# Order and pace of four instruction streams in a two-layer hybrid attention and recurrence block

## The chip, the cores and the metric

The kernel runs on one core of a Trainium2 chip, in one launch. The metric is the device time of that launch in microseconds; a profiled execution gives the span from the first to the last instruction, and every engine's instructions in it.

## What is computed

Two layers run over 512 latent tokens and 256 context tokens of width 1024, in float32. Each layer normalises and modulates the tokens, multiplies them by one wide input matrix, and hands its columns to three groups of heads: latent attention (`mla`), differential attention (`diff`), and a gated recurrence in both directions. The heads' outputs are joined, go through an output matrix, and a gated feed-forward block (`swiglu`) follows.

```python
for l in range(DEPTH):
    h = modulate(rms_norm(x, g_norm1[l]), sh1, sc1)
    fl = stream_features(h, lw, rope)          # h @ w_in, split into head groups
    ...
    mix_l, mix_c = token_mixers(fl, fc, lw, lam, lam_init, with_ctx_out)
    x = x + gt1 * (mix_l @ w_out[l])
    h2 = modulate(rms_norm(x, g_norm2[l]), sh2, sc2)
    x = x + gt2 * swiglu(h2, w_ffn_gate[l], w_ffn_up[l], w_ffn_down[l])
return rms_norm(x, g_final)
```

Layer 0 computes outputs for all 768 tokens, layer 1 for the 512 latent tokens alone; layer 1's keys, values and recurrence states still cover the context.

## The kernel before

Each matrix product is three matmuls (high by high, high by low, low by high part), so every weight block is loaded, copied into its high part on ScalarE (line 102) and subtracted into its low part on VectorE (line 105).

A layer's first phase, `phase_a`, is written as four generators that each put out a few instructions and then yield a cost:

- `g` (`stream_g`): the projections, in the order of a string in `G_ORDER`. `t0` to `t3` are three projections each (forward gate, backward gate, query; called HF, HB and HQ below) that feed head pair 0 to 3 of the recurrence; `h0` and `h1` are the recurrence's values (line 504), `h0` for pairs 0 and 1, `h1` for pairs 2 and 3; `q` is the four blocks of the differential queries and keys, `d` its values; `g0` to `g3` are the output gates of the four pairs; `a4` to `a9` are blocks of the modulation matrix. After the last of them the stream goes on with the output projection, once the recurrence is done.
- `h` (`stream_hh`): the recurrence, two heads side by side (`s` = 0 and 1), four pairs one after another. A pair goes through seven levels (lines 931, 944, 972, 982), then transposes its keys (line 1005), forms chunk states with the values (line 1013), multiplies out (line 1035) and normalises (line 248). The output tiles of a pair wait for its values (`h0` or `h1`). If the pair's gate is there, the pair multiplies it in; else it stores its result in `scr_n`, and the gate step loads it and multiplies.
- `p` (`stream_p`): the low-rank queries, keys and values of latent attention.
- `a` (`stream_a`): attention, which begins where `p` ends. An item is 128 queries of a head: scores (line 775), a reduction (line 779), exponentials, transposes (line 815), and after each two heads a product with the values (line 829). Layer 0 has the units context `mla`, latent `mla` 0, context `diff`, latent `diff` 0, latent `mla` 1, latent `diff` 1, in this order; layer 1 has the latent four.

The streams are interleaved by a virtual clock. `PRM[l]` is the place where `p` begins, and the pace of `g`, `h`, `p` and `a`:

```python
while gens:
    k = min(gens, key=lambda n: vt[n])
    try:
        tc.cur_priority -= AHEAD[l].get(k, 0)
        c = next(gens[k])
        tc.cur_priority += AHEAD[l].get(k, 0)
    ...
    if c == "wait":
        vt[k] = min(vt[o] for o in gens if o != k) + 1e-3
    else:
        vt[k] += c * stretch[k]
```

An instruction's place in this writing order is its priority: of the instructions that are ready by the framework's own costs, the one with the lowest number goes first on its engine, so a late one may still run early as filling. `AHEAD` lowers the number of a stream's instructions by so many places. The matmuls of the levels and of the product with the values have their number lowered by 1000 apart from that. The engines then run their queues in the order so fixed; all loads and stores share SyncE's queue.

The output projection of a layer runs in two batches of tokens (first and second), and its tile `xT` takes the room that the recurrence's tiles leave. The first batch needs the recurrence and the attention of its own tokens; the second batch needs all attention. The feed-forward block behind it does not depend on the strings that change.

Of the kernel before, what the change touches and what calls it, by code (L numbers as in the profile page):

```python
# [31 lines left out]
GROUPS = ((4, 4, 4, 4, 3, 3), (4, 4, 4, 4, 3, 3))  # L32
LEVELS = (1, 2, 4, 8, 16, 32, 64)
PRED = (1, 2, 4, 8, 16)
G_ORDER = ("t0 h0 q t1 d t2 h1 t3 a5 a4 g0 a8 a6 g1 a9 a7 g3 g2", "t0 t1 h0 t2 q d h1 t3 g0 g1 g3 g2")


PRM = ((40, 2, 2.1, 2, 1.2), (45, 1.8, 2.7, 2.2, 0.4))


NQ, NA = 8, 4
# [16 lines left out]
RUSH = 1000  # L58
RUSH2 = 1000
TRB = 0  # L60
AHEAD = ({}, {})
NSTEP = "011"


# [31 lines left out]
def build(tc, I, out):  # L96
# [310 lines left out]
    def hpair():  # L407
        return (hp.tile([128, KT, T], F32R, tag="hh", name="hh"), hp.tile([128, KT, T], F32R, tag="hl", name="hl"))
# [13 lines left out]
    def phase_a(l, h, fs):  # L422
# [92 lines left out]
        def stream_g():  # L515
# [72 lines left out]
            for i in range(2):  # L588
                steps[f"h{i}"] = partial(hi, i)
            for key in G_ORDER[l].split():  # L590
                yield from steps[key]()
# [518 lines left out]
        with ps:  # L1110
            vt = {"g": 0.0, "h": 0.0, "p": PRM[l][0], "a": 1e9}
            apool = ExitStack()
            gens = {"g": stream_g(), "h": stream_hh(),
                    "p": stream_p(apool.enter_context(tc.tile_pool(name=f"P{l}", bufs=1, reuse_waits="tile")))}
            stretch = dict(zip("ghpa", (PRM[l][i] for i in (1, 2, 3, 4))))
# [6 lines that stand above are left out]
                except StopIteration:  # L1122
# [17 lines left out]

    FIRST = {"q": [O_DQ, O_DQ + 128, O_DK], "t": [O_HF, O_HB, O_HQ]}[G_ORDER[0][0]]
    h = hpair()
# [114 lines left out]
    for l in range(DEPTH):  # L1257
# [4 lines left out]
        with ExitStack() as fs:  # L1262
# [9 lines left out]
            def ada_next():  # L1272
                for ll, nb in [(0, 10), (0, 11)] + [(1, nb) for nb in range(12)]:
                    if f"{'ab'[ll]}{nb}" in " ".join(G_ORDER).split():
                        continue
# [332 lines left out]
```

## Time and profile before

| what | before |
| --- | --- |
| median of 3 runs | 2206.95 us (2202.46 to 2211.0) |
| the profiled execution | 2209.03 us, its span 2206.9 us |
| mean granted TensorE clock in it | 0.944 |
| PE busy | 2032.4 us, 92% |
| DVE busy | 1605.8 us, 73% |
| ACT busy | 1060.0 us, 48% |

PE is TensorE's matmuls, DVE is VectorE, ACT is ScalarE, SP is SyncE. "Busy" counts time in which an engine had an instruction of its own in work. The granted clock is a share of full speed, averaged over a stretch. The profiled execution's time is 2.1 us over its span, and 2.1 us over the median.

### The profile page before, as it was taken

Reading aid. Unit: us, or ns where it says so; the run is one execution under the profiler, and the core shown is the slowest. Engines: PE = TensorE matmul, PEld = TensorE weight load, DVE = VectorE, ACT = ScalarE, POOL = GpSimd, SP = SyncE. Lnnn points to the kernel's source line nnn. Section 1 sums busy time; section 2 is a strip of 40 time slices with the busy share of each in tenths; the row PEclk is TensorE's granted clock in tenths of the full one; section 3 lists DMA queues with packets and bytes.
Section 4 is the critical chain, followed back from the end, with each engine's and each line's share of the span. In section 5 each row is a group of like instructions: output and inputs, shape, how many; then the busy total and the mean of one; then the engine's idle time right before and its main releaser. Section 6 shows DMA issues by size and latency. Waiting matters only on the chain. (4 is left out here: it accounts for less than half of the span.)

```text
span 2206.9 us, 38015 instructions
## 1 busy us (share of the span) xinstructions
PE 2032.4 (92%) x14863; PEld 1759.1 (80%) x14863; DVE 1605.8 (73%) x3395; ACT 1060.0 (48%) x1871; POOL 13.1 (1%) x48
## 2 busy tenths in 40 slices
PE   7999899888898999999999999978988699999998
PEld 4887778666678888999999878757866489899997
DVE  5574597888657565797776776798568668877787
ACT  4433778565654323232333454445677444344443
POOL 0000000000000000000000000000000000000000
PEclk7999999888999999999999999989988589999999
DMA  9426744455765424464322333354645263333321
GB/s 318 122 77 165 196 131 131 128 164 170 223 203 167 125 86 153 129 187 132 118 70 68 118 114 102 95 150 128 171 129 163 83 204 98 96 105 101 103 85 68
DMA packets 321243, 296.51 MB, mean 134 GB/s; under 512 B 28875, under 2 KB 263721, under 8 KB 321065
## 3 DMA queue, kind: packets, MB, share of 16 engines
q1 hardware_dynamic: 321064, 294.10, 45.5%
q8 instruction: 117, 1.92, 0.4%
q14 instruction: 62, 0.50, 0.1%
HBM read 241.09 MB, written 52.95 MB: 133 GB/s over the span
## 5 line engine op out<-in xcount | busy, mean ns | idle before, releaser
L102 ACT ACTIVATE whi<-wst 128x1024 fp32r<-128x1024 f32 (+2 forms) x248 | 225.1, 908 | 399.9 <-PE f L195 146.4
L105 DVE TENSOR_TENSOR wlo<-wst,whi 128x1024 fp32r<-128x1024 f32 (+2 forms) x248 | 256.0, 1034 | 80.3 <-ACT whi L102 77.3
L195 PE MATMUL q<-hh,whi 128*128 128x384 f32 (+1 forms) x708 | 222.9, 317 | 4.3 <-ACT whi L102 3.2
L195 PE MATMUL q<-hh,wlo 128*128 128x384 f32 (+1 forms) x708 | 221.2, 315 | 0.9 <-DVE wlo L105 0.9
L195 PE MATMUL q<-hl,whi 128*128 128x384 f32 (+1 forms) x708 | 221.7, 314 | 0.0
L195 PE MATMUL g<-hh,whi 128*128 128x512 f32 (+1 forms) x560 | 199.6, 359 | 10.2 <-ACT zt L102 5.0
L195 PE MATMUL g<-hh,wlo 128*128 128x512 f32 (+1 forms) x560 | 197.8, 355 | 2.1 <-DVE wlo L105 2.1
L195 PE MATMUL g<-hl,whi 128*128 128x512 f32 (+1 forms) x560 | 198.9, 357 | 0.7 <-DVE hl L108 0.5
L195 PE MATMUL f<-ah,whi 128*128 128x512 f32 (+1 forms) x380 | 137.3, 364 | 5.3 <-DVE xT L108 4.1
L779 DVE TENSOR_REDUCE mx<-b 128x1 f32<-128x768 f32 (+1 forms) x120 | 101.5, 848 | 55.3 <-PE b L775 54.4
L195 PEld LDWEIGHTS q<-hh,whi 128*128 128x128 f32 x708 | 134.3, 190 | 9.1 <-ACT whi L102 5.1
L195 PE MATMUL f<-ah,wlo 128*128 128x512 f32 (+1 forms) x380 | 136.1, 361 | 1.1 <-DVE wlo L105 1.1
L195 PE MATMUL f<-al,whi 128*128 128x512 f32 (+1 forms) x380 | 136.5, 361 | 0.0
L108 DVE SCALAR_TENSOR_TENSOR xT<-f,mod,xT 128x256 f32<-128x256 f32 (+1 forms) x164 | 85.9, 546 | 69.1 <-PE f L195 68.5
L195 PEld LDWEIGHTS q<-hh,wlo 128*128 128x128 f32 x708 | 134.3, 190 | 1.7 <-DVE wlo L105 1.6
L195 PEld LDWEIGHTS q<-hl,whi 128*128 128x128 f32 x708 | 134.7, 191 | 0.3
L195 PEld LDWEIGHTS g<-hh,whi 128*128 128x128 f32 x560 | 108.1, 193 | 26.6 <-ACT zt L102 6.1
L102 ACT ACTIVATE kz<-KK 64x384 f32<-64x384 f32 (+1 forms) x192 | 91.3, 476 | 76.1 <-DVE KK L972 55.9
L775 PE MATMUL b<-k,q 96*128 96x256 f32 x352 | 100.5, 399 | 25.8 <-DMA q<-scr_d 15.6
L195 PEld LDWEIGHTS g<-hh,wlo 128*128 128x128 f32 x560 | 107.4, 192 | 17.2 <-DVE wlo L105 3.3
L195 PE MATMUL g<-T,whi 128*128 128x384 f32 (+1 forms) x544 | 121.1, 311 | 0.0
L195 PE MATMUL g<-m,whi 128*128 128x256 f32 (+1 forms) x512 | 117.2, 323 | 4.2 <-ACT acc L102 2.0
(308 smaller groups left out, 5021.2 us busy)
## 6 DMA issues: line engine op xcount, KB each, us to landing
wst<-in_w_in_dram SPq DMA_DIRECT2D x58, 512.0 KB, 5.3
wa<-in_w_ada_dram SPq DMA_DIRECT2D x56, 512.0 KB, 3.8
wst<-in_w_out_dram SPq DMA_DIRECT2D x32, 512.0 KB, 5.5
wst<-in_w_ffn_down_dram SPq DMA_DIRECT2D x64, 256.0 KB, 2.9
wst<-in_w_ffn_gate_dram SPq DMA_DIRECT2D x26, 512.0 KB, 3.7
wst<-in_w_ada_dram SPq DMA_DIRECT2D x24, 512.0 KB, 4.9
hin<-scr_z SPq DMA_DIRECT2D x48, 192.0 KB, 3.4
k<-scr_k SPq DMA_DIRECT2D x16, 576.0 KB
```

Of the source, the lines that this page charges most:

```text
L102: return S.activation(out=out, in_=in_, func=func, **kw)
L105: eng.tensor_tensor(out=out, in0=in0, in1=in1, op=op)
L108: return V.scalar_tensor_tensor(out=out, in0=in0, scalar=scalar, in1=in1, op0=op0, op1=op1)
L195: PE.matmul(out=o, lhsT=x[:, k, ms], rhs=y[:, k, cols], start=start and k == 0 and p == 0, stop=stop and k == nk - 1 and p == 2, skip_grou ...
L775: PE.matmul(out=s[:, 256 + k0:256 + k0 + kn], lhsT=qq[:, q0:q0 + 128], rhs=kk[:, k0:k0 + kn], start=p == 0, stop=p == len(passes) - 1)
L779: V.tensor_reduce(out=mx, in_=sv, axis=AX.X, op=ALU.min)
```

## The change

It sets other constants: the order of the `g` steps in both layers, the pace of `g` and `a` in layer 0, the place where `p` begins in layer 1, and `AHEAD`, which was empty. In layer 0 `h0` moves behind `q` and `t1`, and the gates and modulation blocks at the end change places. In layer 1 `h0` moves in front of `t1`, and `g3` in front of `t3`. Attention's instructions are numbered 80 places earlier in layer 0 and 40 in layer 1, those of layer 1's recurrence 40 places later. Every computation stays.

```diff
-G_ORDER = ("t0 h0 q t1 d t2 h1 t3 a5 a4 g0 a8 a6 g1 a9 a7 g3 g2", "t0 t1 h0 t2 q d h1 t3 g0 g1 g3 g2")
-
-
-PRM = ((40, 2, 2.1, 2, 1.2), (45, 1.8, 2.7, 2.2, 0.4))
+G_ORDER = ("t0 q t1 h0 d t2 h1 t3 a8 a5 a4 a6 g1 a9 g0 a7 g2 g3", "t0 h0 t1 t2 q d h1 g3 t3 g0 g1 g2")
+
+
+PRM = ((40, 2.4, 2.1, 2, 0.91), (35, 1.8, 2.7, 2.2, 0.4))
...
-AHEAD = ({}, {})
+AHEAD = ({'h': 0, 'a': 80}, {'a': 40, 'h': -40})
```

## Rows read from the trace of the kernel before

**Rows 1.** The page's first part: busy time, share, instructions.
```profile
PE 2032.4 (92%) x14863; PEld 1759.1 (80%) x14863; DVE 1605.8 (73%) x3395; ACT 1060.0 (48%) x1871; POOL 13.1 (1%) x48
```

**Rows 2.** Stretches of both first phases; columns in the first line.
```profile
core 0: us, PE busy (x) PEld busy (x) DVE busy (x) ACT busy (x) POOL busy (x), PEclk, DMA share, GB/s
165.00:250.00 85.00, 75.11 (x415) 59.92 (x414) 41.63 (x64) 37.58 (x68) 0.00 (x0) 0.98 0.71 180
...
400.00:550.00 150.00, 123.97 (x1237) 91.76 (x1237) 124.19 (x304) 91.69 (x170) 0.58 (x4) 0.84 0.54 159
...
618.00:708.00 90.00, 83.83 (x485) 70.86 (x485) 65.12 (x148) 44.25 (x78) 0.00 (x0) 0.94 0.55 171
...
1690.00:1766.00 76.00, 47.98 (x352) 37.04 (x353) 53.77 (x137) 40.27 (x79) 0.03 (x1) 0.63 0.32 96
1766.00:1829.00 63.00, 58.19 (x441) 55.04 (x441) 41.74 (x92) 27.88 (x45) 0.00 (x0) 0.91 0.61 186
```

**Rows 3.** Timeline of layer 1 on PE, around h1's end and the output projection's start.
```profile
1577.08 0.28 PE L504 MATMUL g<-whi,hl 128*128 128x256 f32 x1
...
1594.55 0.39 PE L1035 MATMUL c<-QQ,sb 128*64 128x128 f32 x4
...
1752.42 1.97 PE L248 MATMUL c<-ident,rs_y 128*64 128x128 f32 x16 [1.53 <-DVE rs_y L108]
...
1766.36 0.63 PE L195 MATMUL g<-m,whi 128*128 128x256 f32 x2
```

**Rows 4.** Timeline of layer 0: HQ1's end, starts of pairs 1 and 2, last normalisation.
```profile
243.34 0.69 DVE L108 SCALAR_TENSOR_TENSOR zt<-zt,g 128x512 f32<-128x512 f32 x1 [3.43 <-ACT zt L102]
...
260.95 1.17 DVE L972 TENSOR_TENSOR KK<-KK,hin 64x384 f32<-64x384 f32 x2 [0.26 <-PE c L931]
...
356.50 0.96 DVE L105 TENSOR_TENSOR QQ<-hin 128x768 f32<-128x768 f32 x1 [1.11 <-DMA hin<-scr_z]
...
578.58 1.53 PE L248 MATMUL c<-ident,rs_y 128*64 128x128 f32 x24
```

**Rows 5.** Timeline of layer 0, products with the values: four of them.
```profile
412.23 1.08 PE L829 MATMUL b<-pt,v 128*64 128x256 f32 x8 [0.33 <-ACT pt L102]
...
522.16 2.81 PE L829 MATMUL b<-pt,v 128*64 128x256 f32 x24
...
613.30 4.55 PE L829 MATMUL c<-pt,v 128*64 128x256 f32 x24
...
651.77 2.81 PE L829 MATMUL c<-pt,v 128*64 128x256 f32 x24
```

**Rows 6.** Timeline of SP's queue before layer 0's output projection.
```profile
617.89 0.34 SPq L411 DMA_DIRECT2D v<-scr_w  x1
618.27 0.95 SPq L411 DMA_DIRECT2D m<-scr_m  x2
```

**Rows 7.** Groups by line on PE, 618 to 708 us: attention's share.
```profile
L815 PE MATMUL c<-ident,P 128*128 128x128 f32 x24 | 3.3, 274 | 0.0
L829 PE MATMUL c<-pt,v 128*64 128x256 f32 x24 | 2.8, 383 | 0.0
L775 PE MATMUL b<-zt 96*128 96x256 f32 (+1 forms) x8 | 1.9, 341 | 0.0
L775 PE MATMUL b<-k,q 96*128 96x256 f32 (+1 forms) x6 | 1.8, 375 | 0.0
```

**Rows 8.** What PE waited for, 165 to 250 us: total, times, longest.
```profile
PE b L195 <- DVE zt L105: 5.4, 5, 2.2
...
PE g L195 <- ACT zt L102: 3.5, 2, 2.4
```

**Rows 9.** Stretch 400 to 550 us, line 779's reductions alone; columns us, DVE, clock, DMA.
```profile
400.00:550.00 150.00, 19.35 (x21) 0.84 0.54 159
```

**Rows 10.** The page's DMA issues: KB each, median us to landing.
```profile
hin<-scr_z SPq DMA_DIRECT2D x48, 192.0 KB, 3.4
...
scr_z<-zt SPq DMA_DIRECT2D x19, 384.0 KB, 2.4
```

## The prediction

> **What bounds the kernel now.** The page's busy times come first: PE is busy for 92% of the span, but 2206.9 less 2032.4 us still leaves 174 us without a matmul [rows 1]. Where they lie is read from the stretches. In layer 0 PE is idle for 26 of 150 us between 400 and 550, at a mean clock of 0.84, with DVE busy for 124 of the 150. In layer 1 it is idle for 28 of 76 us between 1690 and 1766, at 0.63 [rows 2]. A mean of 0.63 lies between the two levels of 1.2 and 2.4 GHz; (1 − 0.63) × 2, three quarters of that stretch, ran at the low one. So the first phases lose time twice, to idle PE and to the clock behind it, and both stand where recurrence and attention run out of projections that could fill.
>
> What ends each first phase is read from the timeline, backwards. In layer 1 the output projection starts at 1766.4, 13.9 us behind the last normalisation of the recurrence at 1752.4. The recurrence in its turn was held up at `h1`: its last matmul is at 1577.1, and the pair that had waited multiplies out 17.5 us later [rows 3]. In layer 0 the same tie holds to HQ: pair 1 starts 17.6 us behind the step that closes HQ1 (260.95 less 243.34), pair 2 starts on a load of `scr_z`. The recurrence is thus paced by the projections that feed it, and its last normalisation is at 578.6 [rows 4]. Attention in layer 0 is slower than it could be: between 412 and 522 two pairs of heads of the latent `diff` unit take 55 us each, and the last pair, from 613.3 to 651.8, takes 38.5 [rows 5]. It is still running when the output projection starts, and it delays that start: SP's queue takes the load of the last operands `m` behind a load for attention, at 618.3 [rows 6]. So layer 0's output projection starts at about 618, some 39 us behind the normalisation, where layer 1 needs 14.
>
> **The change, step by step.** The number of instructions and transfers is the same; only order moves. Working through the virtual clock gives the new order of writing. In layer 0 HQ3 stands behind 168.6 units of `g`: 337 at a pace of 2, 405 at 2.4. Attention's last item is written at 415 instead of 469, and the recurrence ends at 499 instead of 432. Attention, which was last, is now ahead of the recurrence's last pair and of the gates. In layer 1 attention's last item stays at 259, HQ3 moves from 289 to 299 behind `g3`, and the recurrence ends at 420 instead of 411.
>
> Attention in layer 0, before the output projection. Pairs of heads that took 55 us can go at 38.5, so two of them give 33 us, and more where the faster pace reaches further pairs; attention should end near 600 to 620 instead of 655, in front of the output projection. That stretch, 618 to 708, then loses attention's matmuls: 3.3 + 2.8 + 1.9 + 1.8 = 9.8 us [rows 7], and some of its clock (0.94 of 90 us, 5.4 us short [rows 2]), of which I take 4. Together −14 us; bounds −5, if those matmuls overlap others, and −18.
>
> The price is paid by what attention overtakes. PE work in front of HQ3 grows by the attention done earlier, one to two pairs of 9.8 us: I take +12 on the start of the recurrence's last pair, bounds 0 and +20. `h0` behind `t1`: PE has done the same work at the end of `h0` as before at the end of HQ1, so `h0` ends at about 243, pair 0 multiplies out 17.5 us later, and pair 1 starts at about 265 instead of 261. I count nothing for it, because pair 2 waits for HQ2 at 356 anyway and covers 4 us; without that cover it costs the 4. The four blocks of `q` move away from the low-rank heads, with which they share the four `zt` buffers. Between 165 and 250 PE waits 5.4 and 3.5 us for them [rows 8]; I take −3, bounds −9 and 0. On DVE, attention's reductions now go in front of the recurrence. They are 19.35 us of 400 to 550 [rows 9]; I take +8 for those that fall into the last pair's chain, bounds 0 and +19. The last normalisation then falls at 578.6 + 12 − 3 + 8 = 595.6.
>
> From there to the output projection: `g3` is now the last step and is written behind the recurrence, so pair 3's result goes through `scr_n`. That adds a store and a load, of which the rows show the like at 2.4 and 3.4 us [rows 10]; 13.9 + 5.8 = 19.7. SP's queue has no attention loads in front of the `m` loads any more. The projection starts at 615.3, −2.5 against 617.8. The gates' own matmuls are hidden behind the last pair; if they are not, the gate adds what layer 0 shows now, up to 19 us (39 − 19.7). The modulation blocks only change places among fillers: nothing, unless one falls into the last 20 us.
>
> Layer 0: −2.5 − 14 = −16.5 us, bounds −50 and +14.
>
> Layer 1. `h0` in front of `t1` lets pair 0 finish sooner, but pair 2 waits for `h1`, whose place behind the same work does not move: nothing. `p` begins 10 units earlier and attention 40 places earlier: attention ends some us sooner, −3, since only 4.8 us of idle PE stand in the output projection's stretch [rows 2]. The recurrence is 40 places later, and `g3`, 24 matmuls of 512 columns, stands in front of `t3`; at 58.2 us for 441 matmuls of mostly 256 columns [rows 2] that is 48 × 0.13 = 6 us on the start of the last pair's first head. The end goes through its second head, which waits for pair 2's normalisation, so I take +3. Sum 0, bounds −20 and +15.
>
> The feed-forward blocks are untouched. Against the profiled execution, 2209.0 − 16.5 = 2192.5; it lies 2.1 us over the median of the runs, so 2190 us.
>
> **The rivals.** A difference of 0.5%, 11 us, is what a measurement of this kernel can tell from none.
>
> The recurrence's tail stands alone, 2202 us. With attention done, pair 3 of layer 0 runs with gates and modulation blocks alone. Layer 1's tail shows what a thin stretch is like: 48.0 us of matmuls at 0.63 would be 30.2 at full clock, 17.7 lost in 76. A tail of 50 us like it costs 11.7, the start moves to 627, and of the 16.5 us 4.8 are left. For it: the new order ends so; against it: projections that attention overtook fill up to 450 and later. The Trainium skill, "TensorE: Matmul & The Clock Gate", section "What's actually happening", makes the low clock the default that activity releases; by that rule this rival would be the likelier, and the trace agrees at 0.63.
>
> Nothing moves, 2207 us. Late-numbered work already runs early as filling, and the waits for data may fix the real order. Against it: two pairs at 55 us show that numbers decide.
>
> The recurrence becomes the end of both layers, 2226 us, slower. Its chain yields to attention on DVE and to the projections: with both upper bounds and no gain from `zt`, the normalisation falls at 578.6 + 20 + 19 = 617.6, the start at 637.3; +19.5 − 14 = +5.5. Layer 1 pays the 6 us of `g3` and 8 of reductions, +14. It decides from 612 on: then the start is at 632 and the 14 us are used up. For it: `AHEAD` sets the recurrence back by 80 places against attention in both layers; against it: its matmuls keep their own lead of 1000.
>
> Both layers gain, 2167 us. Layer 0 reaches −22, with the bounds of clock and `zt`; layer 1's tail gets its 17.7 us of clock back, because attention ends before it and DVE is free for the last pair.
>
> **How the numbers follow.** Forecast 0.43, with a range of its own of 2178 to 2200; tail alone 0.20; nothing moves 0.07; slower 0.18; both gain 0.12. Faster by over 0.5%, below 2196: 0.38 of the forecast, 0.12 and 0.03 of the first rival, 0.53. Slower, above 2218: 0.18 and 0.01 of the layers' upper bounds, 0.19. The rest, 0.28, lies within 0.5%. The range is 2162 to 2222: it leaves out half of the slower case and a third of the best one, under 2 in 10.
>
> **What would show it.** Attention's last product with the values in layer 0 before the output projection's first matmul, and pairs of heads near 38 us; `h0` after HQ1; the last normalisation near 596 and the output projection 20 us behind it; that projection's stretch at some 76 us instead of 90; layer 1's output projection at the same distance behind the start of its first phase. The prediction is wrong if the normalisation falls behind 612, if pairs of heads stay at 55 us, or if layer 1's thin stretch grows or vanishes.

## The result, and the profile after

The changed kernel takes 2176.53 us (median, 2176.17 to 2179.02) against 2207.09 us of the kernel before in the same comparison: a ratio of 0.9856, with a 95% interval of 0.9833 to 0.988. It gained 30.6 us where 16.5 were forecast. The outer range (2162 to 2222) held it and the sign was right, but not the place: layer 1, counted at nothing, gave two thirds.

The page's first part after, to be read against [rows 1]:

```profile
span 2175.0 us, 37987 instructions
...
PE 2009.0 (92%) x14863; PEld 1741.4 (80%) x14863; DVE 1603.5 (74%) x3395; ACT 1051.1 (48%) x1859; POOL 13.1 (1%) x48
```

The span is 31.9 us shorter. The same 14863 matmuls were busy for 23.4 us less, and PE idle 8.5 us less (174.5 to 166.0); the execution's mean granted clock rose from 0.944 to 0.962. So about three quarters of the gain is shorter time in the same matmuls, at a higher mean clock, and a quarter is idle time itself.

Whole phases before, to show where the time lay (layer 0's first phase from 50 us on, layer 1's up to the end of `h1`, and from there to the thin stretch of [rows 2]; columns in the first line):

```profile
core 0: us, PE busy (x) PEld busy (x) DVE busy (x) ACT busy (x) POOL busy (x), PEclk, DMA share, GB/s
50.00:708.00 658.00, 596.22 (x5088) 486.47 (x5088) 464.55 (x1061) 381.30 (x692) 2.34 (x16) 0.94 0.55 157
...
579.00:618.00 39.00, 28.51 (x167) 20.55 (x162) 22.57 (x39) 23.95 (x42) 0.00 (x0) 0.78 0.82 251
...
1295.00:1577.00 282.00, 254.85 (x2186) 212.47 (x2185) 213.26 (x485) 144.16 (x277) 1.75 (x12) 0.95 0.47 126
1577.00:1690.00 113.00, 103.54 (x788) 80.41 (x786) 84.14 (x204) 83.18 (x145) 0.55 (x4) 0.91 0.55 156
```

The same stretches after, and those that answer to [rows 2]:

```profile
50.00:697.00 647.00, 589.47 (x5090) 481.01 (x5089) 464.06 (x1062) 375.67 (x682) 2.33 (x16) 0.97 0.56 159
...
400.00:550.00 150.00, 133.79 (x1473) 100.28 (x1473) 133.38 (x310) 104.89 (x193) 0.87 (x6) 0.95 0.53 154
...
583.00:609.00 26.00, 25.25 (x166) 20.96 (x163) 17.52 (x38) 13.16 (x22) 0.00 (x0) 1.00 0.91 280
...
609.00:697.00 88.00, 79.25 (x455) 66.60 (x454) 59.65 (x126) 39.00 (x62) 0.00 (x0) 0.96 0.63 194
...
1286.00:1552.00 266.00, 246.14 (x2157) 206.73 (x2156) 208.68 (x474) 145.37 (x278) 1.75 (x12) 0.97 0.50 133
1552.00:1660.00 108.00, 97.42 (x793) 75.76 (x792) 86.55 (x212) 76.84 (x135) 0.29 (x2) 0.97 0.60 165
1660.00:1736.00 76.00, 49.96 (x374) 37.15 (x375) 54.91 (x141) 42.88 (x86) 0.29 (x2) 0.63 0.35 101
1736.00:1797.00 61.00, 55.60 (x440) 52.85 (x440) 41.69 (x91) 27.78 (x45) 0.00 (x0) 0.95 0.61 180
```

Layer 0's first phase lost 11 us. Between 400 and 550 PE is idle for 16 us instead of 26, at 0.95 instead of 0.84. From the last normalisation to the output projection 26 us pass instead of 39, at a granted clock of 1.00 (2.4 GHz) instead of 0.78, with as many matmuls: the late gates and modulation blocks now stand there. In layer 1 the stretch to the end of `h1` is 16 us shorter (7 of it idle), the next one 5 (all of it time in matmuls, at 0.97 instead of 0.91). The thin stretch before the output projection is as long and as slow as it was, 76 us at 0.63.

The timeline after, with the steps of [rows 3 to 5] (start us, us, engine, line): layer 0's two steps of HQ1 (512 tokens, then 256), the end of `h0`, the starts of pairs 1 and 2, the products with the values, the last normalisation, and the output projection, then layer 1's.

```profile
223.35 0.69 DVE L108 SCALAR_TENSOR_TENSOR zt<-zt,g 128x512 f32<-128x512 f32 x1 [2.73 <-ACT zt L102]
...
229.73 0.41 DVE L108 SCALAR_TENSOR_TENSOR zt<-zt,g 128x256 f32<-128x256 f32 x1
...
253.29 0.28 PE L504 MATMUL g<-whi,hl 128*128 128x256 f32 x1
...
283.11 1.13 DVE L972 TENSOR_TENSOR KK<-KK,hin 64x384 f32<-64x384 f32 x2
...
373.76 1.14 DVE L972 TENSOR_TENSOR KK<-KK,hin 64x384 f32<-64x384 f32 x2 [0.31 <-PE c L931]
...
419.31 2.81 PE L829 MATMUL b<-pt,v 128*64 128x256 f32 x24
...
513.34 2.81 PE L829 MATMUL b<-pt,v 128*64 128x256 f32 x24
...
579.87 3.47 PE L829 MATMUL b<-pt,v 128*64 128x256 f32 x24
...
583.17 1.04 PE L248 MATMUL c<-ident,rs_y 128*64 128x128 f32 x14
...
609.56 0.63 PE L195 MATMUL g<-m,whi 128*128 128x512 f32 x2
...
621.20 2.81 PE L829 MATMUL b<-pt,v 128*64 128x256 f32 x24
...
1551.82 0.28 PE L504 MATMUL g<-whi,hl 128*128 128x256 f32 x1
...
1721.54 0.70 PE L248 MATMUL c<-ident,rs_y 128*64 128x128 f32 x4
...
1736.39 0.63 PE L195 MATMUL g<-m,whi 128*128 128x256 f32 x2
...
1742.78 2.81 PE L829 MATMUL b<-pt,v 128*64 128x256 f32 x24
```

The step of HQ1 that [rows 4] show is its first. The one that closes HQ1 came 7 us behind it in the kernel before, so pair 1 started 10.2 us behind the close there, not 17.6:

```profile
250.79 0.41 DVE L108 SCALAR_TENSOR_TENSOR zt<-zt,g 128x256 f32<-128x256 f32 x1
```

Line 504 also multiplies `d`, right behind `h0`; the line at 253.29 is the 144th of its matmuls, and `h0` has 144.

Attention's last product in layer 0 ends at 624 instead of 655, the normalisation falls at 583 (before 579), the output projection starts at 609.6 (before 617.8). Counted from pair 0's first multiplication in layer 1 (1304.8 before, 1295.5 after), `h1` ends at 256 us instead of 272, the output projection starts at 441 instead of 462 and ends at 501.5 instead of 524.

### The profile page after: what moved, and what is told of

It reads as the page before. It is cut to its first block, busy times and chain, and to the rows that moved or that the text cites. A ratio compares the mean times of both kernels' runs of the same rounds, so it can differ in the third digit from the quotient of the medians.

```text
span 2175.0 us, 37987 instructions
## 1 busy us (share of the span) xinstructions
PE 2009.0 (92%) x14863; PEld 1741.4 (80%) x14863; DVE 1603.5 (74%) x3395; ACT 1051.1 (48%) x1859; POOL 13.1 (1%) x48
## 4 chain that ended last, share of the span: by engine, by line
PE 65%; DVE 22%; DMA 6%; ACT 4%; issue 3%; SPq 1%; DVEq 0%; ACTq 0%
PE g L195 19%; PE q L195 19%; PE f L195 11%; DVE KK L972 3%; DVE QQ L972 3%; DVE sc L982 3%; PE b L775 2%; PE g L504 2%; PE b L195 2%; DVE mx L779 2%; DVE wlo L105 2%; PE b L829 2%; DVE sb L108 2%; DMA q<-scr_q 1%; DVE zt L105 1%
## 5 line engine op out<-in xcount | busy, mean ns | idle before, releaser
L195 PEld LDWEIGHTS g<-hl,whi 128*128 128x128 f32 x560 | 108.1, 194 | 18.0 <-DVE hl L108 2.5
```

What stands on the lines that cost most here:

```text
L195: PE.matmul(out=o, lhsT=x[:, k, ms], rhs=y[:, k, cols], start=start and k == 0 and p == 0, stop=stop and k == nk - 1 and p == 2, skip_grou ...
```

## The experiments

Ratios are to the kernel before on the same chip, with 95% intervals; its medians there were 2210.91, 2211.68 and 2212.66 us. Layer 1's times below 600 are counted from pair 0's first multiplication; larger ones are times in the profile. Each profile is one execution. Ten of the profiled kernels (the one before among them) have the same instructions in the same order in layer 0; its last normalisation lies between 575.6 and 585.4 us in them, its output projection starts between 614.0 and 623.6. So a few us between single executions tell nothing there. Four kernels have layer 1's constants of before; its first phase takes 522.5 to 526.2 us in them.

**Each layer alone.** All of layer 0's constants, with layer 1's as before:

```diff
-G_ORDER = ("t0 h0 q t1 d t2 h1 t3 a5 a4 g0 a8 a6 g1 a9 a7 g3 g2", ...
-PRM = ((40, 2, 2.1, 2, 1.2), ...
-AHEAD = ({}, {})
+G_ORDER = ("t0 q t1 h0 d t2 h1 t3 a8 a5 a4 a6 g1 a9 g0 a7 g2 g3", ...
+PRM = ((40, 2.4, 2.1, 2, 0.91), ...
+AHEAD = ({'h': 0, 'a': 80}, {})
```

> The kernel before with layer 0's constants of the change alone (order, pace of g and a, attention 80 places earlier). In the changed kernel layer 0's first phase ended 10.9 us sooner and layer 1's took some 21 us less. Theory 1, the layers gain apart from each other: 2207 - 11 = 2196 us, with layer 1's first phase as long as before. Rival, layer 1 gains from what layer 0 leaves behind (the numbers of all later instructions stay 80 places lower once attention has ended, which reaches into layer 1): 2207 - 25 to - 31 = 2176 to 2182 us.

2195.5 us, 0.9928 [0.9909, 0.9946]. Layer 0's output projection runs from 607.9 to 692.8, and layer 1's first phase is as long as before (524.8 us, before 524.1).

Layer 1's constants, with layer 0's as before:

```diff
-G_ORDER = (..., "t0 t1 h0 t2 q d h1 t3 g0 g1 g3 g2")
-PRM = (..., (45, 1.8, 2.7, 2.2, 0.4))
-AHEAD = ({}, {})
+G_ORDER = (..., "t0 h0 t1 t2 q d h1 g3 t3 g0 g1 g2")
+PRM = (..., (35, 1.8, 2.7, 2.2, 0.4))
+AHEAD = ({}, {'a': 40, 'h': -40})
```

> The kernel before with layer 1's constants alone (h0 and g3 moved, the low-rank stream beginning at 35, attention 40 places earlier and recurrence 40 later). Theory 1, the layers apart: 2207 - 21 = 2186 us, layer 0's first phase unchanged with its output projection at 618. Rival, layer 1 gains through layer 0: 2200 to 2207 us.

2186.96 us, 0.9893 [0.9873, 0.9913]. Layer 0's output projection starts at 617.9, as before; layer 1's first phase takes 502 us, as in the whole change. So the layers gain apart, and layer 1 more. The two parts multiply to 0.9822, a little under the whole's 0.9856, which the intervals do not settle. In the profiles layer 0's output projection ends 4.3 us later in the whole (697.1) than with layer 0's constants alone (692.8), less than the ten executions above differ there (704.2 to 713.8).

**Layer 0, taken apart.** The order alone (the first string of `G_ORDER`), and pace with numbering alone (`PRM` and `AHEAD`, the old order):

```diff
-G_ORDER = ("t0 h0 q t1 d t2 h1 t3 a5 a4 g0 a8 a6 g1 a9 a7 g3 g2", ...
+G_ORDER = ("t0 q t1 h0 d t2 h1 t3 a8 a5 a4 a6 g1 a9 g0 a7 g2 g3", ...
```

> The kernel before with layer 0's order of projections alone. Theory 5, as the prediction has it, layer 0 gains through attention's pace and numbering, and its order gives 3 us by fewer waits for the zt buffers and loses as much by h0: within 0.3% of before. Rival, the order gives layer 0's gain of 0.7%: -0.5% or more.

2227.91 us, 1.0068 [1.0051, 1.0084]: slower. Timeline of that kernel: HQ1's first step, the last normalisation, the last gate step, the output projection's start.

```profile
219.20 0.69 DVE L108 SCALAR_TENSOR_TENSOR zt<-zt,g 128x512 f32<-128x512 f32 x1
...
610.95 0.77 PE L248 MATMUL c<-ident,rs_y 128*64 128x128 f32 x10
...
626.31 0.41 DVE L108 SCALAR_TENSOR_TENSOR zt<-zt,g 128x256 f32<-128x256 f32 x1
...
635.82 0.63 PE L195 MATMUL g<-m,whi 128*128 128x512 f32 x1
```

HQ1's first step comes 24 us sooner than in [rows 4], and the last pair starts at 457.2 (before 455.2), but it normalises 32 us later; the gates follow it, and the output projection starts 18 us later. Attention ends at 676, 21 us later. Why the last pair takes 30 us more was not found.

```diff
-PRM = ((40, 2, 2.1, 2, 1.2), ...
-AHEAD = ({}, {})
+PRM = ((40, 2.4, 2.1, 2, 0.91), ...
+AHEAD = ({'h': 0, 'a': 80}, {})
```

> The kernel before with layer 0's paces (g 2.4, a 0.91) and attention 80 places earlier, its order as before. Theory 5: -0.5 to -0.8%, attention's pairs of heads of the latent diff unit near 40 us instead of 55, its end 30 us sooner. Rival, without the order it gains nothing, as layer 1's parts did: within 0.2%, or slower.

2248.31 us, 1.0164 [1.0142, 1.0186]: the slowest kernel of the study. The same steps, with pair 1's start:

```profile
283.93 0.69 DVE L108 SCALAR_TENSOR_TENSOR zt<-zt,g 128x512 f32<-128x512 f32 x1 [1.84 <-ACT zt L102]
...
299.43 1.12 DVE L972 TENSOR_TENSOR KK<-KK,hin 64x384 f32<-64x384 f32 x2
...
628.47 0.91 PE L248 MATMUL c<-ident,rs_y 128*64 128x128 f32 x6 [0.84 <-DVE rs_y L108]
...
658.53 0.62 PE L195 MATMUL g<-m,whi 128*128 128x512 f32 x2
```

With `h0` still in front of `t1`, attention overtakes `t1`: two of its products with the values (250.6 and 274.2) stand in front of HQ1's first step, where the first one before (253.4) stood behind it. From 165 to 250 PE also idles for 19 us instead of 10, at 0.85 instead of 0.98. HQ1's first step comes 41 us later than before, pair 1 starts 38 later, the normalisation falls 50 later and the output projection starts 41 later. Attention itself ends at 673, 18 us later and not 30 sooner. The order takes this away: with it, under the same pace, HQ1's first step is at 223. So +1.6% and +0.7% alone make −0.7% together.

**Layer 1, one edit at a time.** The place where `p` begins:

```diff
-PRM = (..., (45, 1.8, 2.7, 2.2, 0.4))
+PRM = (..., (35, 1.8, 2.7, 2.2, 0.4))
```

> The kernel before with one number changed: layer 1's low-rank stream begins at 35 instead of 45. Theory 1, the earlier start of attention is what layer 1 gains by (its first reduction came 41 us sooner in the changed kernel, and its end 31): 2207 - 15 to - 21 = 2186 to 2192 us. Rival A, the order of the projections is: 2204 us, since 10 units at 1.8 to 2.2 a unit are one step of g. Rival B, the priorities are: 2207 us.

2221.6 us, 1.0038 [1.0021, 1.0056]. `h1` does end sooner, 259 us behind the layer's first multiplication, and the normalisation falls at 1741.1 instead of 1752.4, but attention ends later. Timeline of its output projection's start and attention's last product:

```profile
1759.40 0.50 PE L195 MATMUL g<-m,whi 128*128 128x256 f32 x2
...
1792.44 4.50 PE L829 MATMUL b<-pt,v 128*64 128x256 f32 x24 [0.90 <-ACT pt L102]
```

The projection starts 7 us sooner than in [rows 3], its first batch is done at 1788.7, and its second runs from 1810.5 to 1838.5, behind attention: 79 us instead of 62.5. My theory, that the earlier start alone is the cause, fell.

The numbering alone, and both together:

```diff
-AHEAD = ({}, {})
+AHEAD = ({}, {'a': 40, 'h': -40})
```

> The kernel before with layer 1's numbering alone (attention 40 places earlier, recurrence 40 later). Theory 3, numbering is what makes the earlier start pay: alone it takes the recurrence's time and gives attention's, -0.2 to +0.3%. Rival, numbering alone makes attention faster and is worth -0.5% or more by itself.

2208.59 us, 0.9993 [0.9972, 1.0014]: nothing that the runs can tell, though layer 1's first phase takes 518.7 us in its profile.

```diff
-PRM = (..., (45, 1.8, 2.7, 2.2, 0.4))
-AHEAD = ({}, {})
+PRM = (..., (35, 1.8, 2.7, 2.2, 0.4))
+AHEAD = ({}, {'a': 40, 'h': -40})
```

> The kernel before with the earlier start of the low-rank stream and the numbering of layer 1 together, its order as before. Theory 3, the two belong together: the start alone cost 0.4%, together they gain 0.3% (layer 1's whole part less its order), so 2204 us beside 2211, and attention's pairs of heads take 30 to 37 us instead of up to 49. Rival, they do not belong together: the start's loss stays, +0.2 to +0.5%, and the part's gain beyond the order comes from the order with one of them.

2197.83 us, 0.9939 [0.9919, 0.996]. `h1` ends at 257, the normalisation falls at 439, and attention's last product begins at 461 (469 in the kernel before, 487 with the start alone). So the start brings `h1` forward, and the numbering lets attention keep up with it; neither is worth anything alone.

The order alone, and its two moves one by one (`h0` ahead of `t1`; `g3` ahead of `t3`):

```diff
-G_ORDER = (..., "t0 t1 h0 t2 q d h1 t3 g0 g1 g3 g2")
+G_ORDER = (..., "t0 h0 t1 t2 q d h1 g3 t3 g0 g1 g2")
```

> The kernel before with layer 1's order of projections alone (h0 in front of t1, g3 in front of t3). Theory 1, the earlier start of attention is the cause: no gain here, 2207 us, or some 5 us more, since g3 sits in front of the last pair's projections. Rival A, the order is the cause (pair 0 finishes without a wait for h0, so pair 1 and 2 come earlier and h1 after them): 2207 - 15 = 2192 us. Rival B, the priorities are: 2207 us.

2193.09 us, 0.9922 [0.9901, 0.9943]. `h1` ends where it did (270, before 272); the gain lies behind it. Pair 3's first head takes 62 us from its first multiplication to its key transposes (75 before), and the output projection starts at 1754.8 and ends at 1814.1, with attention done at 1764.

```diff
+G_ORDER = (..., "t0 h0 t1 t2 q d h1 t3 g0 g1 g3 g2")
```

> The kernel before with h0 in front of t1 in layer 1, and nothing else. Theory 2: within 0.2% of before, since pair 2 still waits for h1. Rival: -0.6 to -0.8%, with the starts of pairs 1 and 2 some 10 us earlier.

```diff
+G_ORDER = (..., "t0 t1 h0 t2 q d h1 g3 t3 g0 g1 g2")
```

> The kernel before with g3 in front of t3 in layer 1, and nothing else. Theory 2, the order gains in the tail: one gate fewer stands among the last pair's levels and attention's last items, so that pair takes some 62 us instead of 75 from its first multiply to its key transposes; then this edit holds nearly the whole gain of the order, -0.6 to -0.8%. Rival, h0 in front of t1 is what counts, by an earlier pair 0: no change here, or +0.2% for the last pair's later start.

1.001 [0.9991, 1.0029] and 0.9992 [0.9972, 1.0012]: nothing each. In both the normalisation falls at 440 to 442 (before 448), and attention's last product begins 7 to 8 us later (476, before 469; 457 with the whole order). With `g3` alone pair 3's first head takes 62 us, as Theory 2 had it, but it starts 10 us later (335, before 325); with both moves it starts at 327, so `h0` takes that delay away. With `g3` alone the output projection starts at 455, seven sooner, and then takes 71 us. The timeline there, on SP's queue and PE:

```profile
1754.59 1.47 SPq L411 DMA_DIRECT2D m<-scr_m  x3
1758.71 0.33 SPq L411 DMA_DIRECT2D k<-scr_d  x1
1759.08 0.45 SPq L411 DMA_DIRECT2D q<-scr_d  x1
...
1759.46 0.79 PE L195 MATMUL g<-m,whi 128*128 128x256 f32 x2 [0.78 <-DMA m<-scr_m]
...
1780.30 1.08 PE L829 MATMUL b<-pt,v 128*64 128x256 f32 x7 [0.55 <-ACT pt L102]
```

Attention's last operands `k` and `q` are issued behind loads of `m`, which wait for the recurrence.

**Is it the queue?** Layer 1's loads of `m` and `xT` are set behind attention's last load of `q` in SP's queue, on top of `g3` alone and of the earlier start alone (the load of `q` and one of `m` are shown, `xT`'s is changed likewise):

```diff
-        nc.sync.dma_start(out=out_, in_=in_)
+        return nc.sync.dma_start(out=out_, in_=in_).ins
...
-                load(q, sq[:, :, q0:q0 + 256].rearrange("i r t -> r i t"))
+                last_q[0] = load(q, sq[:, :, q0:q0 + 256].rearrange("i r t -> r i t"))
...
-                        load(m2[:, k], scr_m[l][k, :, :, cols].rearrange("i p t -> p i t"))
+                        with ExitStack() if full else tc.issue_after(last_q[0]): load(m2[:, k], scr_m[l][k, :, :, cols].rearrange("i p t -> p i t"))
```

> g3 in front of t3 as in the run of that edit alone, and in layer 1 the loads of m and xT for the output projection are put behind attention's last load on SP's queue; up to there the kernel's queues are the same. Theory 4, that load's place is why the edit alone gained nothing: the recurrence ended 8 us sooner, but attention's last load of k stood behind five m loads and attention ended 6 us later. Then k goes out at about 1749 instead of 1758.7, attention ends some 10 us sooner, the output projection starts at the same time or up to 3 us later and takes some 60 us instead of 71: -0.4 to -0.7% against the kernel before. Rival, attention is slow there by DVE or by its buffers and the load's place is a symptom: within 0.2% of the kernel before.

2206.83 us, 0.9974 [0.9958, 0.9989], 0.2% under `g3` alone. SP's queue in that kernel:

```profile
1755.40 0.32 SPq L411 DMA_DIRECT2D k<-scr_d  x1
1755.77 0.44 SPq L411 DMA_DIRECT2D q<-scr_d  x1
1756.31 4.76 SPq L411 DMA_DIRECT2D m<-scr_m  x8
```

`k` is issued only 3 us sooner, and attention's last product begins 3 us sooner; the output projection starts 5 us later and takes 60 us. Counted from pair 0's first multiplication `k` is 7 us sooner (447, before 454), but the load of `v` in front of it, up to which the queues are the same, is 6 us sooner already (434, before 440).

> The earlier start of layer 1's low-rank stream alone, which cost 0.4%, with the same order of loads as in the run beside it. Theory 4: attention's last load goes out at about 1762 instead of 1770, and its second last pair is not touched; the gain is some 8 to 15 us, so -0.3 to 0% against the kernel before. Rival: the loss of 0.4% stays.

2222.1 us, 1.0048 [1.0031, 1.0064], no better than the start alone; attention's last load of `k` goes out at 1772.3, not at 1762 (1770.0 with the start alone), and its last product begins at 1794.9. So the queue is a small part of what the `g3` edit lost, and no part of what the earlier start lost. Why attention falls behind in the single edits was not settled.

## Why the prediction was right in its range and wrong in its steps

**What bounds the kernel** was read rightly in the main: each first phase ends with the chain from the projections through the recurrence to the output projection, and attention counts where it reaches into it. The gain came from idle PE and from time in the same matmuls, as the argument had it: PE's busy time fell by 23.4 us.

That the time fell into the range is in part luck: layer 0 gave less than its forecast, and layer 1, counted at nothing, made up for more than that. The forecast's own range, 2178 to 2200, missed by 1.5 us. One bound of the working does not come out of its terms either: the lower ones of layer 0 add up to −46.5, not −50 (−9 on the normalisation, 28.5 us before 617.8 at the projection's start, and −18).

One reading was wrong as well. The load of `m` at 618.3 [rows 6] can't have delayed layer 0's output projection, for the projection was already running:

```profile
617.77 0.74 PE L195 MATMUL g<-m,whi 128*128 128x512 f32 x2
```

**Layer 0: −10.9 us measured (617.8 to 609.6 and 90.2 to 87.5), −16.5 forecast.** The sign held; the terms were mis-sized, and attention came sooner by another way than the one forecast.

- *Attention before the output projection* (−14). Attention came 31 us sooner, but not because pairs of heads that took 55 us went at 38.5: the two before 522 took 57.6 and 52.3 us and now take 47.4 and 52.3, and the last one takes 41.3 (before 38.5). Attention began sooner: its first scores are at 217.9 instead of 237.7, and its second product with the values is 34 us ahead (250.3, before 284.5). That the forecast end (600 to 620) nearly came out is luck. And its last pair still ran until 624, inside the projection. Groups on PE there, 609 to 697 us, against [rows 7]:

```profile
L829 PE MATMUL b<-pt,v 128*64 128x256 f32 x24 | 2.8, 383 | 0.0
L815 PE MATMUL b<-ident,P 128*128 128x128 f32 x12 | 1.7, 278 | 1.2 <-DVE P L108 1.2
L775 PE MATMUL b<-k,q 96*128 96x256 f32 (+1 forms) x4 | 1.2, 370 | 0.0
```

  5.7 us are left of 9.8. PE's busy time in the stretch fell by 4.6 us and its idle time rose by 2.6, so the term was worth some 2 to 3 us, less than the bound of −5.
- *The price on the recurrence* (+17: 12 − 3 + 8). The normalisation moved by 4.6 us, to 583.2, within what executions with layer 0 as before show (575.6 to 585.4). The last pair began 6.5 us later (461.7, before 455.2) and took 121.5 us from there, before 123.4, although DVE was busier from 400 to 550 (133 us, before 124). The terms +12 and +8 were far too high.
- *`h0` behind `t1`* (nothing). HQ1 closed 21 us sooner (229.7, before 250.8), but `h0` ended at 253.6 instead of the 243 worked out, pair 0 multiplied out 22 us behind that (275.4) instead of 17.5, and pair 1 started at 283 instead of 265. Pair 2 started at 374 (before 357.5). That need not be this delay passed on: pair 2 starts 14 us behind HQ2's second step (359.5), and did so 11 us behind it before (346.9), so HQ2 itself came late. At the last pair 6.5 us are left. That the move had no cost or gain of its own was wrong in another way: without the new string, under the new pace, the normalisation falls at 628. The parts of layer 0 were added as if independent, and they are not.
- *The wait for `zt` buffers* (−3). PE's two waits of [rows 8] from 165 to 250, 5.4 and 3.5 us in total, became these (total, count, longest), 1.8 us less together. The rows name the instruction on `zt` that PE waited for; that a lack of `zt` buffers held it is not shown.

```profile
PE b L195 <- DVE zt L105: 4.3, 3, 2.7
...
PE g L195 <- ACT zt L102: 2.8, 1, 2.8
```

- *From the normalisation to the output projection* (19.7). It took 26.4: the late gates and blocks stand there, at the full clock, and SP's queue still has loads for attention among those of `m` (`k` at 599.2). It is 12.8 us better than before, not the 19.5 forecast.

**Layer 1: −22.6 us measured, 0 forecast.** This is the step that failed: "pair 2 waits for `h1`, whose place behind the same work does not move: nothing". `h1`'s place in the string did not move, but its end came 16 us sooner: the low-rank projections begin earlier, and PE idles 7 us less, at 0.97 instead of 0.95. The runs with the earlier start show this (259, 257 and 257); the order alone does not (270). From `h1` to the output projection another 5 us went (189.3 to 184.6), and 2 in the projection itself. The run with the order alone shows that `g3` and `h0` pay there together, where `g3` was counted at +3 and `h0` at nothing. Attention's last product begins 21 us sooner (447, before 469); for the projection that was worth the 2 us, near the −3 forecast. In both pairs the edits need each other, which a sum of single costs can't show; 0.9939 for one pair and 0.9922 for the other make 0.9861, where the whole layer measured 0.9893, so they may overlap as well, which the intervals do not settle.

**The rivals.** "The recurrence's tail stands alone" did not happen: layer 0's stretch from 583 to 609 ran at 1.00. The Trainium skill's rule behind it ("TensorE: Matmul & The Clock Gate", section "What's actually happening", that the low clock is the default and activity releases it) agrees with the rows: PE was busy for 25.3 of those 26 us, and in layer 1's thin stretch for 50.0 of 76, at 0.63. "The recurrence becomes the end", the slower rival, is what layer 0 does without its order: the normalisation at 628 is past the 612 from which it was to decide, and the time was 36 us longer. The way was another one: 41 of the 50 us are there at HQ1's first step, in the projections that feed the chain. "Both layers gain" was nearest in result, 2167, but by another way: layer 1's thin stretch got none of its clock back. The measured time lies between it and the forecast, just under the forecast's own range.

## What to carry to other kernels

Edits to order and pace of streams that are interleaved in one phase don't add: here −0.7% was made of +0.7% and +1.6%, and −0.6% of +0.4% and nothing, so a forecast has to ask of each edit what it overtakes under the others. Look first at what feeds the chain that sets the end (here `t1` and `h1`): the pace of another stream pays only as long as that feed keeps its lead. A recurrence that ends sooner gains nothing if the other consumer of the same phase, attention, ends later.

## What the runs showed of the hardware

Matmul time is not a constant of the work: the same 14863 matmuls were busy for 2032.4 us before, 2009.0 after and, with layer 0's pace and numbering alone, 2057.4, in one execution each. With the work unchanged, the order of issue moved the time in matmuls by 2.4%; the mean granted clocks are 0.944, 0.962 and 0.937. I had counted 4 us of clock; 23.4 of the 31.9 us gained are time in matmuls, and 8.5 are idle time.
